# A hybrid decoder step on one core: wider transfers for the triangular inverses, convolution taps and state updates moved from GpSimd to VectorE, and narrow float32r products padded to 128 rows

## The chip, the cores and the metric

The kernel runs on one core of a Trainium2 chip. The metric is the time of one execution on the device, in microseconds. TensorE (PE) multiplies matrices, VectorE (DVE), ScalarE (ACT) and GpSimd (POOL) work on elements, and SyncE (SP) issues every DMA of this kernel. Results of TensorE go to PSUM, whose contents VectorE and ScalarE read.

## The reference, cut to what matters

One inference step of a two-layer decoder for a prompt of 512 tokens and 8 sample tokens, model width 2048, all in float32. Layer one holds a 31-tap convolution module and stick-breaking attention, the latter also over paged caches of 2048 past tokens for each of the 8 samples. Layer two is a gated DeltaNet with 16 query/key heads and 32 value heads of dimension 128. Both layers begin with one large input projection and end with an output projection, a residual and a layer norm.

The change is mostly in layer two. Its core, for the prompt in chunks and for the samples in one recurrent step, is:

```python
qkv, new_buf = _causal_depthwise_conv(qkv, conv_buf, conv_w)      # 4 taps, 8192 channels
qkv = silu(qkv)
# prompt: per chunk of c tokens
lmat = where(strict, einsum('bhnid,bhnjd->bhnij', kb, kc) * decay, 0.0)
tmat = triangular_solve(lmat + eye, eye, lower=True, unit_diagonal=True)
...
# samples: one step with the state s (8 samples, 32 heads, 128 x 128)
s = s * exp(g_t)[..., None, None]
delta = (v_t - einsum('bhkv,bhk->bhv', s, k_t)) * b_t[..., None]
s = s + einsum('bhk,bhv->bhkv', k_t, delta)
o = einsum('bhkv,bhk->bhv', s, q_t)
```

## The kernel before, in words

**Planner.** `build` doesn't call the engines directly. Each operation is recorded (`Sched.record`) with its dependencies, a cost from `Sched.cost` and a priority, and `Sched.flush` simulates the five engines and emits the operations in the order of the start times that it worked out. There is a flush at the end of each stage. On the chip every engine then runs its own list in that fixed order, and real semaphores hold it where an input is late. `sc.prio` shifts a priority; `-HP` comes first. SP's list holds every DMA, so a DMA that takes long to issue delays the ones behind it.

**Projections.** `gemm` loads a weight block (512 KB, `wr`), splits it into a high and a low part of type float32r (`wh` by ScalarE, `wl` by VectorE), splits the activations the same way (`uh`, `ul`), and adds up three products in PSUM (`pg`). These matmuls of 128 rows and 260 columns make up most of TensorE's work.

**Layer two.** The second flush region begins with `gates` and then `prepare(i)` for the 16 head pairs: two projections, a 4-tap convolution of each (`conv_c`), the products of keys with keys and queries (`kqh`, `kql`), a broadcast of the cumulated gates (`gr`, a product of `idr`, one column repeated, with `gst`, 64 rows), and the stores of what the scan needs into DRAM, tiles `sp0` to `sp15` (kq, kt, it, lt). Slots 5 and 6 of the seven hold the triangular matrices of the pair's two value heads.

**Inverses.** `inverses(b8, iv)` takes eight head pairs at once. It loads the 64 x 64 diagonal blocks of their triangular matrices, one block per partition (8 pairs x 2 heads x 4 chunks x 2 blocks = 128), into the tile `m`, inverts them on VectorE by 119 multiply-and-reduce steps (`tmp<-m`, then `m<-tmp`), and stores the blocks back. Batch 0 runs beside the preparation of pairs 8 to 15 and the first gate projections (`z`); batch 1 is a generator that is advanced in the background of the scan (`background`). Batch 1 uses the same tile `m`.

**Scan.** The next flush region goes over the 16 pairs: `values(i)` (two projections and `conv_c` for the values), `z_gates`, `scan(i)` (loads the four chunks `pk` from `sp`, finishes the inverse on TensorE and steps the prompt's state through the chunks), `samples(i)` (the recurrent step of the 8 samples), `normalise(i)` and the store of `y`. The tiles of this stage (`lb`: `oss`, `es`, `selr`, ...) take the memory that the preparation's tiles (`lk`) held, among them the `dd` buffers through which the gates `z` are stored.

**Samples.** `samples(i)` loads the pair's state `S` (1 MB), multiplies it on TensorE by a selection of keys and queries (`es`), sums the four column groups by `selr` (8 columns of weights, twice two products), works out the deltas on 8 partitions, replicates them with `repr` (8 rows, two products) into `dm`, and adds the outer products (`kx` x `dm`, 32 rows, two samples at a time into the PSUM tile `pl`, of which there is one buffer) to the state, which GpSimd has multiplied by the decay `egb` in one operation of 2048 columns. Then `S` is stored (`o_ds`) and its only buffer is free for the next pair.

**Other places.** In layer one, `scores(b)` replicates a query row by a product of 40 rows and 512 columns (`sel8`, `qrow`; 16 times in all), and `bcast_half` broadcasts four statistics columns by a product of 4 rows.

Of the kernel before, what the change touches and what calls it, by code (L numbers as in the profile page):

```python
# [38 lines left out]
class Sched:  # L39
# [79 lines left out]
    def region(self, ap):  # L119
# [24 lines left out]
        return rec, p0, p0 + dims[0][1], m  # L144

# [83 lines left out]
    def cost(self, eng, meth, args, kw, out, ins):  # L229
# [21 lines left out]
        if eng == "SP":  # L251
# [8 lines left out]
            few = any(x.space != bass.MemoryType.DRAM and x.shape[0] <= 8 for x in [out] + ins) and by > 20000  # L260
# [223 lines left out]
def build(tc, a, ctx):  # L484
# [173 lines left out]
    with ExitStack() as l0:  # L658
# [89 lines left out]
        qrow = lp.tile([40, H, P], F32R, name="qrow")  # L748
        sel8 = lp.tile([40, NB], F32R, name="sel8")
        S.copy(sel8, ident[0:40, 40:48])  # L750
        for j in (0, 32):
            S.copy(sel8[j:j + NB], ident[j:j + NB, j:j + NB])
        for g in range(2):
# [4 lines left out]
            S.copy(qg, qp[0:40])  # L758
# [464 lines left out]
    spill = [dr.tile([4, P, 7, P], F32, name=f"sp{i}") for i in range(GQ)]  # L1223
# [3 lines left out]
    with ExitStack() as l1:  # L1227
# [14 lines left out]
        idr = kp.tile([2 * NH, NH], F32R, name="idr")  # L1242
# [8 lines left out]
        def conv_c(g, psf, dst, win, s):  # L1251
# [30 lines left out]
        def prepare(i, lk):  # L1282
# [126 lines left out]
        def gates(gp_):  # L1409
# [28 lines left out]
            S.copy(gst, gc2)  # L1438
# [37 lines left out]
        with ExitStack() as l1a:  # L1476
            lk = sc.pool(l1a, "l1a", 1)
            gst = lk.tile([2 * NH, T], F32R, name="gst")
# [71 lines left out]
        selr = lb.tile([P, 2, NB], F32R, name="selr")  # L1550
        S.copy(selr, C("sel_kq").rearrange("p (j b) -> p j b", j=2))
        repr_ = lb.tile([NB, 2, 32], F32R, name="repr")
        S.copy(repr_, C("rep8", NB).rearrange("p (j r) -> p j r", j=2))
# [89 lines left out]
        def samples(i, dv, oss, lb):  # L1643
# [25 lines left out]
            qs = lb.tile([NB, 2, P], F32, name="qs")  # L1669
            for hd in range(2):  # L1670
                h = 2 * i + hd
                V.scalar_tensor_tensor(dl[:, hd, :], kp_[:, 0, hd, :], rows8[:, 0, h:h + 1], vr[:, hd, :], op0=ALU.mult, op1=ALU.add)
                V.tensor_scalar(dl[:, hd, :], dl[:, hd, :], rows8[:, 1, h:h + 1], None, op0=ALU.mult)
                S.activation(qs[:, hd, :], kp_[:, 1, hd, :], AF.Copy, scale=rows8[:, 2, h:h + 1])
            V.scalar_tensor_tensor(qs, dl, qk8[:, i:i + 1], qs, op0=ALU.mult, op1=ALU.add)
            for hd in range(2):
                V.scalar_tensor_tensor(vr[:, hd, :], qs[:, hd, :], 1.0 / P, qs[:, hd, :], op0=ALU.mult, op1=ALU.mult,
                                       accum_out=oss[0:NB, 8 + hd:9 + hd])

            dh = lb.tile([NB, 2, P], F32R, name="tmp1")  # L1680
            S.copy(dh, dl)
            dlo = lb.tile([NB, 2, P], F32R, name="el")
            V.tensor_tensor(dlo, dl, dh.bitcast(F32), op=ALU.subtract)
            rp = pm.tile([32, 256], F32, name="pd", bufs=1)
            for j, x in enumerate((dh, dlo)):
                PE.matmul(rp, repr_[:, j], x.rearrange("p h v -> p (h v)"), start=(j == 0), stop=(j == 1))
            dm = lb.tile([32, 256], F32R, name="dm")
# [3 lines left out]
            G.tensor_tensor(s, s, egb[:, :, 2 * i:2 * i + 2, None].broadcast_to([P, NB, 2, P]), op=ALU.mult)  # L1691
            for b2 in range(NB // 2):
                if b2 % 2 == 0:
                    kx = lb.tile([32, 4, P], F32R, name="kx")
                    V.tensor_tensor(kx, kw[:, None, :].broadcast_to([32, 4, P]),
# [4 lines left out]
                sv = s[:, 2 * b2:2 * b2 + 2].rearrange("p b h v -> p b (h v)")  # L1700
                V.tensor_tensor(sv, sv, up, op=ALU.add)
# [3 lines left out]
        def normalise(i, osb, qs, oss, zt, y, lb):  # L1705
# [16 lines left out]
            V.tensor_tensor(qs, qs, oss[0:NB, 8:10, None].broadcast_to([NB, 2, P]), op=ALU.mult)  # L1722
            op_ = pm.tile([P, 2, NB], F32, name="pd", bufs=1)
            for hd in range(2):
                PE.transpose(op_[:, hd, :], qs[:, hd, :], ident[0:NB, 0:NB])
# [194 lines left out]
```

## Time and profile before

| | |
|---|---|
| median of 3 runs | 3327.67 us (3323.73 to 3341.83) |
| the profiled execution | 3313.89 us |
| its span, first to last instruction | 3312.1 us |
| TensorE busy | 3108.7 us, 94% |
| VectorE busy | 2341.9 us, 71% |
| ScalarE busy | 1566.5 us, 47% |
| GpSimd busy | 342.6 us, 10% |
| DMA | 667.02 MB, mean 201 GB/s |

The span is what the rows of the trace are counted in. The profiled execution is faster than the median by 13.8 us. Busy time is a union of spans; matmuls are pipelined, so that a span reaches beyond the time at which the next one starts, and a TensorE at 94% is not at its peak. Layer one lies from 0 to about 1280 us, the preparation from there to about 1870, the scan from 1920 to about 2925, and the last projection behind it.

### The profile page before, as it was taken

To read this page: it belongs to the slowest core of one execution; us is meant where nothing else is said; L and a number is where in the kernel's file an instruction comes from. 1 tells how busy PE (TensorE), PEld (TensorE's weight loads), DVE (VectorE), ACT (ScalarE), POOL (GpSimd) and SP (SyncE) were. 2 spreads that over 40 slices of the span, in tenths; PEclk is the share of its full clock that TensorE was granted. 3 is DMA by queue.
4 is the path that set the end of the run, shared out by engine and by line. 5 is a ranking of instruction groups with operands and counts; after the bars stand their busy time and mean duration, and the time that the engine had idled before them with its cause. 6 is when DMAs were issued, how large, how long until landed. Compare 5 with 4: busy or idle time off the path is not lost. (4 is left out here: it accounts for less than half of the span.)

```text
span 3312.1 us, 65624 instructions
## 1 busy us (share of the span) xinstructions
PE 3108.7 (94%) x24496; PEld 2806.7 (85%) x24496; DVE 2341.9 (71%) x6214; ACT 1566.5 (47%) x2927; POOL 342.6 (10%) x301
## 2 busy tenths in 40 slices
PE   8999999989979999999999668999989999999997
PEld 5898888877867777999999667987878989999997
DVE  3487989787864485668999426998975766566755
ACT  2234344434552366777652124545444655554544
POOL 0000000000001011111110011111112110101111
PEclk9999999999979999999999888998989999999999
DMA  9978989998538886776653255544446545376764
GB/s 317 298 256 290 316 299 315 304 319 305 175 119 282 296 294 210 162 163 151 146 151 116 74 113 145 140 141 145 139 126 186 149 145 161 119 231 211 225 185 139
DMA packets 361586, 667.02 MB, mean 201 GB/s; under 512 B 103697, under 2 KB 216338, under 8 KB 357170
## 3 DMA queue, kind: packets, MB, share of 16 engines
q1 hardware_dynamic: 361266, 662.82, 65.4%
q8 instruction: 193, 3.16, 0.4%
q14 instruction: 127, 1.04, 0.1%
HBM read 574.95 MB, written 87.70 MB: 200 GB/s over the span
## 5 line engine op out<-in xcount | busy, mean ns | idle before, releaser
L418 PE MATMUL pg<-uh,wh 128*128 128x260 f32 (+1 forms) x6112 | 1343.9, 289 | 6.6 <-ACT uh L418 3.1
L418 PE MATMUL pg<-ul,wh 128*128 128x260 f32 (+1 forms) x6112 | 1339.8, 289 | 1.5 <-DVE ul L418 1.1
L418 PEld LDWEIGHTS pg<-uh,wh 128*128 128x128 f32 (+1 forms) x6112 | 998.3, 190 | 62.2 <-issue 46.6
L418 PEld LDWEIGHTS pg<-ul,wh 128*128 128x128 f32 (+1 forms) x6112 | 998.9, 190 | 56.1 <-issue 43.6
L418 PE MATMUL pg<-uh,wl 128*128 128x260 f32 (+1 forms) x6112 | 892.0, 289 | 0.0
L418 DVE TENSOR_TENSOR wl<-wr,wh 128x1024 fp32r<-128x1024 f32 (+3 forms) x508 | 618.7, 1218 | 382.6 <-PE pg L418 161.5
L418 ACT CAST wh<-wr 128x1024 fp32r<-128x1024 f32 (+3 forms) x508 | 511.4, 1007 | 791.9 <-PE pg L418 671.3
L418 PEld LDWEIGHTS pg<-uh,wl 128*128 128x128 f32 (+1 forms) x6112 | 793.2, 190 | 46.6 <-issue 39.2
L418 DVE SCALAR_TENSOR_TENSOR junk<-page,qbc 128x128 f32<-128x128 f32 x1024 | 222.6, 284 | 9.7 <-ACT qbc L418 6.2
L418 DVE TENSOR_TENSOR tmp<-m 128x224 f32<-128x224 f32 (+19 forms) x238 | 214.5, 901 | 4.5
L418 DVE SCALAR_TENSOR_TENSOR acc<-gp,conv_w_a,acc 128x512 f32<-128x512 f32 x240 | 181.0, 754 | 6.6 <-ACT acc L418 3.9
L418 ACT ACT_TABLE_LOAD x120 | 154.0, 1283 | 49.8 <-DVE rs L418 19.5
L418 DVE TENSOR_REDUCE m<-tmp 128x32 f32<-128x224 f32 (+19 forms) x238 | 130.7, 549 | 3.3
L418 POOL TENSOR_SCALAR ctap<-buf,conv_w_c 128x512 f32<-128x512 f32 x64 | 72.7, 1135 | 524.9 <-ACT buf L418 521.5
L418 POOL TENSOR_TENSOR cacc<-cacc,ctap 128x512 f32<-128x512 f32 x64 | 84.9, 1326 | 388.6 <-DVE cacc L418 340.8
L418 DVE SCALAR_TENSOR_TENSOR cacc<-buf,conv_w_c,cacc 128x512 f32<-128x512 f32 x128 | 99.9, 781 | 13.9 <-ACT cacc L418 9.6
L418 PE MATMUL pl<-wa,cpad 128*32 128x512 f32 x512 | 81.0, 604 | 5.8 <-DMA wa<-w_ada 5.6
L418 DVE DVE_READ_ACCUMULATOR junk<-page,qbc 128x1 f32 x1024 | 81.4, 79 | 0.0
L418 PE MATMUL pg<-yh,wh 128*128 128x260 f32 x320 | 79.1, 283 | 0.0
L418 PE MATMUL pg<-yl,wh 128*128 128x260 f32 x320 | 78.9, 283 | 0.0
L418 POOL TENSOR_TENSOR S<-S,egb 128x2048 f32<-128x2048 f32 x16 | 59.5, 3722 | 165.4 <-PE pd L418 165.4
L418 PE MATMUL pl<-page,wst 128*32 128x512 f32 x512 | 75.1, 611 | 0.2
(377 smaller groups left out, 3615.5 us busy)
## 6 DMA issues: line engine op xcount, KB each, us to landing
wr<-w_in_odd SPq DMA_DIRECT2D x194, 512.0 KB
page<-cache_k SPq DMA_DIRECT2D x128, 512.0 KB
wa<-w_ada SPq DMA_DIRECT2D x128, 512.0 KB
page<-cache_v SPq DMA_DIRECT2D x128, 512.0 KB
wr<-w_out_odd SPq DMA_DIRECT2D x128, 512.0 KB
wr<-w_in_even SPq DMA_DIRECT2D x94, 512.0 KB
page<-w_ada SPq DMA_DIRECT2D x128, 256.0 KB
pk<-sp SPq DMA_DIRECT2D x64, 448.0 KB
```

The lines of the kernel that those rows point to most:

```text
L418: o[2](*o[3], **o[4])
```

## The change

- `inverses` loads and stores blocks of 16 partitions (four head pairs, one value head, one diagonal block) instead of 4; the order of blocks on the partitions changes with it. For this the sixteen DRAM tiles `sp` become one tile `spa` of which `spill[i]` are slices, and the planner's `region` learns which parts of it an access touches. The planner's price for transfers of few partitions now holds up to 16 partitions.
- `conv_c` runs its three taps on VectorE; the GpSimd product and addition are gone.
- `samples` scales and adds the state in one VectorE operation per sample and head (16 of 128 columns per pair) instead of one GpSimd product and four additions.
- Products with fewer than 128 rows get operands with zero rows up to 128: `sel8`/`qrow`, `idr`/`gst`, the statistics broadcast, `repr` (its two products become one, with the low part on rows 32 to 39), `kx`/`dm`, and the transposes of `qs`. `selr` becomes 128 columns wide and one matrix for keys and queries, so that two products do the work of four. The fills are ScalarE copies with scale 0, made once.

```diff
@@ record / region / cost
-            return rec, lo, hi + 1, 1
+            return rec, lo, hi + 1, self.parts(rec["shape"], dims, off) if len(rec["shape"]) == 4 else 1
-            few = any(x.space != bass.MemoryType.DRAM and x.shape[0] <= 8 for x in [out] + ins) and by > 20000
+            few = any(x.space != bass.MemoryType.DRAM and x.shape[0] <= 16 for x in [out] + ins) and by > 20000
+    def parts(self, shape, dims, off):
+
+        per = shape[1] * shape[2] * shape[3]
+        dims = tuple(d for d in dims if d[0] % per)
+        key = (off % per, dims, "parts")
+        if key not in self.masks:
+            idx = np.array([off % per])
+            for s, c in dims:
+                idx = (idx[:, None] + s * np.arange(c)[None, :]).reshape(-1)
+            p, s, f = np.unravel_index(idx, shape[1:])
+            self.masks[key] = sum(1 << int(q) for q in np.unique((p // 64 * shape[2] + s) * 2 + f // 64))
+        return self.masks[key]
@@ bcast_half
-            PE.matmul(out[:, 256:260], col[0:4, 4 + n:5 + n].broadcast_to([4, P]), ident[0:4, 0:4], start=True, stop=True)
+            PE.matmul(out[:, 256:260], col[:, 4 + n:5 + n].broadcast_to([P, P]), ident[:, 0:4], start=True, stop=True)
@@ qrow, sel8, scores
-        qrow = lp.tile([40, H, P], F32R, name="qrow")
-        sel8 = lp.tile([40, NB], F32R, name="sel8")
-        S.copy(sel8, ident[0:40, 40:48])
+        qrow = lp.tile([P, H, P], F32R, name="qrow")
+        sel8 = lp.tile([P, NB], F32R, name="sel8")
+        S.activation(sel8, ident[:, 0:NB], AF.Copy, scale=0.0)
+        S.activation(qrow.rearrange("p h d -> p (h d)"), wst.rearrange("p g q r -> p (g q r)"), AF.Copy, scale=0.0)
...
-                PE.matmul(qp.rearrange("p j d -> p (j d)"), sel8[:, b:b + 1].broadcast_to([40, P]),
+                PE.matmul(qp.rearrange("p j d -> p (j d)"), sel8[:, b:b + 1].broadcast_to([P, P]),
@@ layer two
-    spill = [dr.tile([4, P, 7, P], F32, name=f"sp{i}") for i in range(GQ)]
+    spa = dr.tile([4 * GQ, P, 7, P], F32, name="sp")
+    spill = [spa[4 * i:4 * i + 4] for i in range(GQ)]
...
-            tap = lw.tile([P, T], F32, name="ctap")
-            G.tensor_scalar(tap, buf[:, 0:T], cwc[:, g, 0:1], 0.0, op0=ALU.mult, op1=ALU.add)
-            for t in (1, 2):
+            for t in range(3):
                 V.scalar_tensor_tensor(acc, buf[:, t:t + T], cwc[:, g, t:t + 1], acc, op0=ALU.mult, op1=ALU.add)
-            G.tensor_tensor(acc, acc, tap, op=ALU.add)
...
-                PE.matmul(gr.rearrange("p c f -> p (c f)"), idr[:, h:h + 1].broadcast_to([2 * NH, P]), gst, start=True, stop=True)
+                PE.matmul(gr.rearrange("p c f -> p (c f)"), idr[:, h:h + 1].broadcast_to([P, P]), gst, start=True, stop=True)
@@ inverses
-            for blk in range(2):
-                for i in range(8):
+            for i in (0, 4):
+                for blk in range(2):
                     for hd in range(2):
-                        p0 = blk * 64 + i * 8 + hd * 4
-                        dv = spill[8 * b8 + i][:, blk * 64:blk * 64 + 64, 5 + hd, blk * 64:blk * 64 + 64]
-                        blocks.append((m[p0:p0 + 4], dv))
+                        p0 = 64 * blk + 32 * hd + 4 * i
+                        c0, r = 4 * (8 * b8 + i), slice(64 * blk, 64 * blk + 64)
+                        blocks.append((m[p0:p0 + 16], spa[c0:c0 + 16, r, 5 + hd, r]))
@@ before the scan: selr, repr, kx, dhl, qs made once, filled with zeros
-        selr = lb.tile([P, 2, NB], F32R, name="selr")
-        repr_ = lb.tile([NB, 2, 32], F32R, name="repr")
+        fresh = lambda t, n: S.activation(t, zero.broadcast_to([P, n]), AF.Copy, scale=0.0)
+        selr = lb.tile([P, P], F32R, name="selr")
+        repr_ = lb.tile([P, P], F32R, name="repr")
+        kx = lb.tile([P, 4, P], F32R, name="kx")
+        dhl = lb.tile([P, 2, P], F32R, name="dhl")
+        qs = lb.tile([P, 2, P], F32, name="qs")
@@ samples
-            kp_ = pm.tile([NB, 2, 2, P], F32, name="pd", bufs=1)
-            for j in range(2):
-                for x in (eh, el):
-                    PE.matmul(kp_[:, j].rearrange("p h v -> p (h v)"), selr[:, j], x, start=(x is eh), stop=(x is el))
+            kp_ = pm.tile([P, 2, P], F32, name="pd", bufs=1)
+            for x in (eh, el):
+                PE.matmul(kp_.rearrange("p h v -> p (h v)"), selr, x, start=(x is eh), stop=(x is el))
...
-            for j, x in enumerate((dh, dlo)):
-                PE.matmul(rp, repr_[:, j], x.rearrange("p h v -> p (h v)"), start=(j == 0), stop=(j == 1))
+            PE.matmul(rp, repr_, dhl.rearrange("p h v -> p (h v)"), start=True, stop=True)
...
-            G.tensor_tensor(s, s, egb[:, :, 2 * i:2 * i + 2, None].broadcast_to([P, NB, 2, P]), op=ALU.mult)
...
-                sv = s[:, 2 * b2:2 * b2 + 2].rearrange("p b h v -> p b (h v)")
-                V.tensor_tensor(sv, sv, up, op=ALU.add)
+                for b in (2 * b2, 2 * b2 + 1):
+                    for hd in range(2):
+                        V.scalar_tensor_tensor(s[:, b, hd], s[:, b, hd], egb[:, b, 2 * i + hd:2 * i + hd + 1],
+                                               up[:, b % 2, P * hd:P * hd + P], op0=ALU.mult, op1=ALU.add)
@@ normalise
-                PE.transpose(op_[:, hd, :], qs[:, hd, :], ident[0:NB, 0:NB])
+                PE.transpose(op_[:, hd, :], qs[:, hd, :], ident)
```

## Rows read from the trace of the kernel before

**Rows 1.** Stretches: us; busy us (instructions) of each engine, clock, DMA share, GB/s

```profile
1520.00:1857.00 337.00, 335.44 (x2750) 329.65 (x2750) 324.30 (x582) 172.28 (x247) 34.19 (x39) 0.99 0.52 136
1924.00:2003.00 79.00, 68.17 (x486) 64.62 (x487) 20.45 (x25) 20.68 (x35) 7.33 (x8) 0.87 0.54 122
2003.00:2424.00 421.00, 390.43 (x2977) 351.96 (x2976) 387.01 (x835) 212.10 (x564) 62.68 (x45) 0.92 0.50 144
2424.00:2520.00 96.00, 80.51 (x632) 74.35 (x631) 47.37 (x114) 42.63 (x116) 11.06 (x10) 0.92 0.47 126
2520.00:2925.00 405.00, 396.69 (x3133) 361.38 (x3132) 277.00 (x673) 236.54 (x637) 59.16 (x46) 0.98 0.53 156
```

**Rows 2.** Timeline of VectorE: start us, duration us, operation [idle before, released by]

```profile
1856.10 0.91 DVE L418 MEMSET m<- 128x1024 f32 x1 [0.16 <-issue]
...
1918.12 0.10 DVE L418 MEMSET oss<- 128x10 f32 x2 [56.42 <-DMA z<-dd]
...
2011.39 0.17 DVE L418 TENSOR_TENSOR tmp<-m 128x8 f32<-128x8 f32 x1
```

**Rows 3.** Timeline of SP's queue, 1857 to 2003 us

```profile
1857.03 55.06 SPq L418 DMA_DIRECT2D sp<-m  x31
1912.19 1.56 SPq L418 DMA_DIRECT2D z<-dd  x1
...
2002.79 0.33 SPq L418 DMA_DIRECT2D m<-sp  x1
```

**Rows 4.** Timeline of TensorE behind the hole

```profile
1924.24 1.11 PE L418 MATMUL pm<-ct,vc 128*128 128x128 f32 x4 [52.31 <-ACT vc L418]
```

**Rows 5.** Timeline of SP's queue, the stores of batch 1

```profile
2423.86 3.19 SPq L418 DMA_DIRECT2D sp<-m  x3
...
2508.32 2.16 SPq L418 DMA_DIRECT2D S<-state_delta  x1
...
2513.40 1.19 SPq L418 DMA_DIRECT2D sp<-m  x1
```

**Rows 6.** DMA queue: packets, MB, share; 1875 to 1910, then 1300 to 1302

```profile
q1 hardware_dynamic: 5023, 1.27, 21.7%
...
q1 hardware_dynamic: 1140, 0.57, 98.5%
```

**Rows 7.** VectorE's groups, 2003 to 2424: count, busy us, mean ns, idle before

```profile
L418 DVE SCALAR_TENSOR_TENSOR cacc<-buf,conv_w_c,cacc 128x512 f32<-128x512 f32 x24 | 20.5, 853 | 0.3 <-ACT cacc L418 0.2
L418 DVE TENSOR_TENSOR S<-S,pl 128x512 f32<-128x512 f32 x28 | 18.9, 674 | 0.2 <-PE pl L418 0.2
...
L418 DVE SCALAR_TENSOR_TENSOR st<-st,gl,pm 128x128 f32<-128x128 f32 x42 | 12.7, 339 | 1.6 <-PE pm L418 1.5
...
L418 DVE COPY es<-kqd 128x8 f32<-128x8 f32 x15 | 8.1, 556 | 0.3 <-PE pd L418 0.2
```

**Rows 8.** GpSimd's groups, 2003 to 2424

```profile
L418 POOL TENSOR_TENSOR S<-S,egb 128x2048 f32<-128x2048 f32 x7 | 26.9, 3846 | 26.7 <-PE pd L418 26.7
```

**Rows 9.** Timeline of TensorE around a gate row product and a kx pair

```profile
1391.39 0.40 PE L418 MATMUL pg<-ul,wh 128*128 128x260 f32 x2
1391.63 0.28 PE L418 MATMUL pg<-uh,wh 128*128 128x260 f32 x1
1391.84 0.49 PE L418 MATMUL pd<-gst,idr 64*128 64x512 f32 x1
1392.26 0.39 PE L418 MATMUL pg<-uh,wh 128*128 128x260 f32 x1
1392.49 0.40 PE L418 MATMUL pg<-ul,wh 128*128 128x260 f32 x2
...
2642.40 0.50 PE L418 MATMUL pl<-dm,kx 32*128 32x256 f32 x2
2642.83 0.52 PE L418 MATMUL pg<-ul,wh 128*128 128x260 f32 x2
```

**Rows 10.** TensorE's groups, 1924 to 2925: the kx products

```profile
L418 PE MATMUL pl<-dm,kx 32*128 32x256 f32 x128 | 37.0, 373 | 20.6 <-DVE oss L418 9.4 <-DVE S L418 8.5 <-DVE osb L418 2.0
```

More of the change, by code (lines that the diff above doesn't have):

```diff
@@ L757, in build @@
             qg = qrow[:, g * 4:g * 4 + 4, :]
[L758 removed]
+            S.copy(qg[0:40], qp[0:40])
             V.tensor_tensor(qg[32:40], qp[32:40], qg[32:40].bitcast(F32), op=ALU.subtract)
@@ L1241, in build @@
         rq2 = kp.tile([P, GQ, 4], F32, name="rq2")
-        idr = kp.tile([2 * NH, NH], F32R, name="idr")
+        idr = kp.tile([P, NH], F32R, name="idr")
+        S.activation(idr, ident[:, 0:NH], AF.Copy, scale=0.0)
         kqd = kp.tile([P, GQ, 2, NB], F32, name="kqd")
@@ L1437, in gates @@
             Q.dma_start(gc2[lo], gcs)
-            S.copy(gst, gc2)
+            S.activation(gst, C("mask2").bitcast(F32)[:, 0:1].broadcast_to([P, T]), AF.Copy, scale=0.0)
+            S.copy(gst[0:2 * NH], gc2)
             V.tensor_tensor(gst[lo], gc2[lo], gst[lo].bitcast(F32), op=ALU.subtract)
@@ L1477, in build @@
             lk = sc.pool(l1a, "l1a", 1)
-            gst = lk.tile([2 * NH, T], F32R, name="gst")
+            gst = lk.tile([P, T], F32R, name="gst")
             gates(lk)
@@ L1549, in build @@
             G.memset(t, 0.0)
-        selr = lb.tile([P, 2, NB], F32R, name="selr")
-        S.copy(selr, C("sel_kq").rearrange("p (j b) -> p j b", j=2))
-        repr_ = lb.tile([NB, 2, 32], F32R, name="repr")
-        S.copy(repr_, C("rep8", NB).rearrange("p (j r) -> p j r", j=2))
+        zero = C("mask2")[:, 0:1]
+        fresh = lambda t, n: S.activation(t, zero.broadcast_to([P, n]), AF.Copy, scale=0.0)
+        flat3 = lambda t: t.rearrange("p j f -> p (j f)")
+        selr = lb.tile([P, P], F32R, name="selr")
+        fresh(selr, P)
+        repr_ = lb.tile([P, P], F32R, name="repr")
+        fresh(repr_, P)
+        for j in range(2):
+            S.copy(selr[:, 32 * j:32 * j + NB], C("sel_kq")[:, NB * j:NB * j + NB])
+            S.copy(repr_[32 * j:32 * j + NB, 0:32], C("rep8", NB)[:, 32 * j:32 * j + 32])
+        kx = lb.tile([P, 4, P], F32R, name="kx")
+        fresh(flat3(kx), 4 * P)
+        dhl = lb.tile([P, 2, P], F32R, name="dhl")
+        qs = lb.tile([P, 2, P], F32, name="qs")
+        for t in (dhl, qs):
+            fresh(flat3(t), 2 * P)
         def scan(i, vs, osb, oss, lb):
@@ L1675, in samples @@
-            V.scalar_tensor_tensor(qs, dl, qk8[:, i:i + 1], qs, op0=ALU.mult, op1=ALU.add)
+                S.activation(qs[0:NB, hd, :], kp_[32:32 + NB, hd, :], AF.Copy, scale=rows8[:, 2, h:h + 1])
+            V.scalar_tensor_tensor(qs[0:NB], dl, qk8[:, i:i + 1], qs[0:NB], op0=ALU.mult, op1=ALU.add)
             for hd in range(2):
-                V.scalar_tensor_tensor(vr[:, hd, :], qs[:, hd, :], 1.0 / P, qs[:, hd, :], op0=ALU.mult, op1=ALU.mult,
+                V.scalar_tensor_tensor(vr[:, hd, :], qs[0:NB, hd, :], 1.0 / P, qs[0:NB, hd, :], op0=ALU.mult, op1=ALU.mult,
@@ L1687, in samples @@
-            dm = lb.tile([32, 256], F32R, name="dm")
+            S.copy(dhl[0:NB], dl)
+            V.tensor_tensor(dhl[32:32 + NB], dl, dhl[0:NB].bitcast(F32), op=ALU.subtract)
+            rp = pm.tile([P, 256], F32, name="pd", bufs=1)
+            PE.matmul(rp, repr_, dhl.rearrange("p h v -> p (h v)"), start=True, stop=True)
+            dm = lb.tile([P, 256], F32R, name="dm")
             S.copy(dm, rp)
@@ L1690, in samples @@
             Q.dma_start(kw, krd[:, i, :])
-            G.tensor_tensor(s, s, egb[:, :, 2 * i:2 * i + 2, None].broadcast_to([P, NB, 2, P]), op=ALU.mult)
             for b2 in range(NB // 2):
                 if b2 % 2 == 0:
-                    kx = lb.tile([32, 4, P], F32R, name="kx")
-                    V.tensor_tensor(kx, kw[:, None, :].broadcast_to([32, 4, P]),
+                    V.tensor_tensor(kx[0:32], kw[:, None, :].broadcast_to([32, 4, P]),
                                     C("mask_b", 32)[:, 2 * b2:2 * b2 + 4, None].broadcast_to([32, 4, P]), op=ALU.mult)
@@ L1721, in normalise @@
                                        _pn(zt[hd])[:, :, 0:256], op0=ALU.mult, op1=ALU.mult)
-            V.tensor_tensor(qs, qs, oss[0:NB, 8:10, None].broadcast_to([NB, 2, P]), op=ALU.mult)
-            op_ = pm.tile([P, 2, NB], F32, name="pd", bufs=1)
+            V.tensor_tensor(qs[0:NB], qs[0:NB], oss[0:NB, 8:10, None].broadcast_to([NB, 2, P]), op=ALU.mult)
+            op_ = pm.tile([P, 2, P], F32, name="pd", bufs=1)
             for hd in range(2):
-                PE.transpose(op_[:, hd, :], qs[:, hd, :], ident[0:NB, 0:NB])
+                PE.transpose(op_[:, hd, :], qs[:, hd, :], ident)
             for hd in range(2):
-                V.scalar_tensor_tensor(d8(y[hd]), as8(op_[:, hd, :]), gnw, d8(zt[hd]), op0=ALU.mult, op1=ALU.mult)
+                V.scalar_tensor_tensor(d8(y[hd]), as8(op_[:, hd, 0:NB]), gnw, d8(zt[hd]), op0=ALU.mult, op1=ALU.mult)
         def values(i):
```

9 lines of the change are left out of this document (1 added, 8 removed).

## The prediction

> **What bounds the kernel now.** I read the table of stretches first, then the timelines of the places where it shows a hole, then the groups by shape. The stretches [rows 1] show the change's territory, layer two. While head pairs 0 to 15 are prepared, TensorE is busy 335 of 337 us and VectorE 324: VectorE runs the first batch of triangular inverses beside the preparation, and both engines are full. From 2003 to 2424 us (head pairs 0 to 7 scanned, second batch of inverses in the background) VectorE has 387 of 421 us and TensorE 390. From 2520 to 2925 (pairs 8 to 15, no inverses) TensorE has 397 of 405 and VectorE only 277. Between these lie two poor stretches, 1924 to 2003 (TensorE 68 of 79, VectorE 20) and 2424 to 2520 (81 of 96 and 47).
>
> The hole itself stands between the first two stretches. Batch 0's last operation, a memset, ends at 1857 [rows 2]; from then on SP issues 31 of its 32 stores back to back for 55 us, and the store of the last gate tile, z, stands behind them at 1912 [rows 3]. The second stage's tiles reuse that gate tile's memory, so VectorE waits 56.42 us for it to land [rows 2], and TensorE, out of work at 1872, waits 52.31 us [rows 4]. Then batch 1's 32 loads go out among the weight loads until 2003 [rows 3], and its first multiply runs only at 2011.39 [rows 2]. At the other end of batch 1 the 32 stores take from 2424 to 2513, and the state load of pair 8, which starts the next stretch, comes at 2508 [rows 5].
>
> **The change part by part.** *Transfers.* A store is now 4 partitions of 64 x 64 floats: 256 runs of 256 bytes, 32 stores, 8192 packets. In 35 us amid the hole 5023 packets went, 143 per us, at a DMA share of 21.7%, which is 3.5 of 16 engines [rows 6]: four engines work, close to full, at 28 ns a packet. The stores of preparation, which span 128 partitions, show 570 packets per us at 98.5% [rows 6], again 28 ns per packet and engine, and those packets are twice as large. So the limit is the engine's time per packet, and a transfer of 16 partitions that spreads over 16 engines should carry 8192 packets in 8192/570 = 14.4 us instead of 57. Bounds: 14.4 us, and 57 us if the four engines are not what limits. I take 16, near the row with the same time per packet. The Trainium skill (SBUF — State Buffer, Door 1: The DMA port swizzle) says that four consecutive partitions share one of 16 ports, so 16 of them reach only four; at its 435 GB/s for all ports that would be an estimated 109 GB/s, and 19 us for these 2.1 MB. By it the hole would shrink 3 us less; no run here shows it.
>
> *Resumption.* Before, z goes out at 1912.19 and VectorE resumes at 1918.12, 5.9 us later [rows 2, 3]. After: 1857 + 16 + 5.9 = 1879, 39 us sooner, if batch 0 ends when it did. It ends later by the VectorE work added to the eight pairs beside it (16 convolutions x 0.85 us = 13.6) and sooner by what GpSimd's locks and the gate products give back; I take 3 us later, so 36 us. Five fills on ScalarE now stand before the first convolution of this stage, 1280 columns in all; at 512 columns per 0.85 us they are 2 us, inside the rounding.
>
> *Loads.* The eight new loads carry the same 8192 packets; interleaved with weights I allow 25 us (bounds 16 and 93) from the resumption to the first multiply of batch 1, where it was 93.3 (1918.12 to 2011.39). Batch 1 starts near 1907, 104 us sooner.
>
> *VectorE takes GpSimd's work.* Per pair: two convolutions with one more tap, 2 x 0.85 = 1.7 us, and the state update, 16 multiply-adds of 128 columns at 0.339 (nearest row: st, same operands) = 5.4 in place of 4 x 0.674 = 2.7 [rows 7]. So +4.4. Given back: what GpSimd blocked. The 15 copies es of 8 columns average 0.556 us [rows 7] where another operation on 8 columns takes 0.17 [rows 2], and GpSimd's own product lasts 3.8 us [rows 8]; that is 0.8 per pair, bounds 0 and 8 (all of GpSimd's 62.7 us in this stretch [rows 1]). I take +3.5 per pair, 25 over the seven pairs that ran beside batch 1. At 92% busy the batch then needs 412 + 27 = 439 us, from 1907 to 2346 instead of 2424: 78 us sooner. Its stores, 84 us from their start to pair 8's state load, need 16 plus what SP interleaves; with 20 to 84 as bounds I take 45. VectorE alone would let pair 8 start 78 + 39 = 117 us sooner.
>
> *TensorE.* A narrow product pays three times. The gate row product of 512 columns starts 0.21 us after the matmul ahead (dense: 0.12), takes 0.42, and the next one needs 0.23 [rows 9]: 0.62 us more than if it weren't there. Full rows: 512 columns at the dense 0.12 per 260 is 0.24. Saved 0.38, for 32 of them, and for 16 of the same shape in layer one. A pair of kx products takes 0.43 for two [rows 9] and, with the same 0.20 of switching, 0.63 against 0.24: 0.39 saved, four times per head pair. The two repr products become one (0.41 each at most by the same rows, against 0.12: 0.7), four selr become two (0.24). Together 2.5 us a head pair. Here a rule speaks against the change: the Trainium skill (TensorE: Matmul & The Clock Gate, Why this matters for your kernels) says that a single K=32 matmul takes as long as a K=128 one and that the gain lies in running such tiles side by side. By it only the switching, 0.20 each, would be saved, and this term would halve to some 1.2 us a pair. The trace disagrees: 0.42 for 512 columns at 64 rows against a dense 0.12 for 260.
>
> TensorE's own bound for pairs 0 to 7: its 539 busy us from 1924 to 2520 [rows 1] less 8 x 2.5 = 519, from 1888 on at its 98% of the last stretch, ends 2418 instead of 2520: 102 us. Two engines both near full, each executing in a fixed order, will not reach either bound, 117 or 102; I take **85 us** up to pair 8, which holds all terms so far. Its bounds are 36 (the hole alone) and 102.
>
> *Pairs 8 to 15.* TensorE bounds, 8 x 2.5 = 20 us; VectorE has 128 us to spare for its +28. But each state update now holds the one PSUM buffer for 4 x 0.339 = 1.36 us where it held it 0.67, and kx products already waited 20.6 us [rows 10]. I take **15**, bounds 0 and 20.
>
> *Layer one.* 16 products of qrow x 0.38 = **6**, bounds 0 and 10 with the statistics broadcasts of 4 rows, whose cover is that TensorE is the full engine there. The extra zero rows cost fills on ScalarE, once each, ScalarE being half busy (212 of 421) [rows 1]. One DRAM tile for all pairs instead of sixteen I cost at nothing: the stores of one tile already go out back to back without waiting for landings [rows 3].
>
> Sum: 85 + 15 + 6 = 106 us. The profiled execution is 3313.89 us (span 3312.1), 13.8 below the median of the runs, 3327.67. Counted from the profile that is 3208; I forecast the median, 3327.67 - 106 = 3222 us. On its own this case runs from 3185 (102 + 20 + 10) to 3245.
>
> **The rivals.** *Only the hole closes.* Batch 1 starts sooner but VectorE, with more work in the stage where it is full already, gives nothing more: 36 + 15 + 6 = 57, 3270 us. For it: VectorE and TensorE are both over 90% in that stage. Against it: VectorE had 20 us of work in the 79 from 1924, time that batch 1 can now use.
>
> *The transfers stay as slow.* If the limit is common to all engines, hole, loads and end of batch 1 stay, VectorE's +27 stands against TensorE's 21: 3305 to 3340, no change. The 21.7% speaks against it.
>
> *The state update stalls TensorE (slower).* The mechanism: one PSUM buffer, which TensorE needs again after four VectorE operations instead of one; kx products stand in order ahead of the dense ones. The worst price is that all four rounds of 1.36 + 0.4 us are waited out, 7 us a pair, 113 us in 16, and VectorE's +27 in the first half: 3327.67 - 106 + 140 = 3360. It decides from 106/16 = 6.6 us a pair. Against it: the same ping-pong at half the length cost 20.6 us in all, 1.3 a pair.
>
> **How the numbers follow.** Chances: forecast 0.63, only the hole 0.20, transfers as slow 0.09, stalled update 0.08. The likeliest gives 3222. The range 3170 to 3290 holds the first two and a little beyond the first one's bounds; it leaves out the last two, 0.17. A measurement here tells from no change about 0.5%, 17 us. Faster: 0.63 + 0.20 + 0.01 of the third = 0.84; same 0.08; slower 0.08.
>
> **What would show it right or wrong.** Right: 8 stores that leave SP within some 16 us with DMA share near full, VectorE's wait for z under 15 us, batch 1's first multiply within 30 us of the resumption, pair 8's state load some 85 us sooner, and dense spacing of 0.12 us around the former narrow products. Wrong: stores still of 55 us in sum at a share of 22%; VectorE at 95% or more with TensorE below 90% in pairs 0 to 7; idle time ahead of kx several us a pair. A new order of the work, which the kernel's planner works out from its own costs, could also move layer one by more than the 6 us that I give it.

## The result, and the profile after

The changed kernel took 3224.11 us (median of 4 runs, 3205.37 to 3229.8) beside 3325.7 for the kernel before (4 runs, 3319.95 to 3341.83): ratio 0.9674, 95% interval 0.9629 to 0.972, so faster by 102 us. The forecast was 3222. Run again five times, beside a kernel before of 3312.67 us, it gave 0.9704 (0.9686 to 0.9721). The profiled execution took 3229.8 us, its span is 3228.0: 84 us below the profile of before. It is the slowest of its four runs, and the profile of before (3313.89) is faster than all four runs beside it, so the profiles hold 84 of the 102 us. Two single runs of kernels further down, of 10190.62 and 3290.12 us, show a granted clock of 0.27 and 0.87 where the other runs of the same kernels have 0.97 or more; they enter no ratio and move the medians by less than 1 us. The total came out as forecast; its parts did not.

The table of stretches, cut where the rows of before were cut [rows 1] (us, then busy us and count of each engine, granted clock, DMA share, GB/s):

```profile
1504.00:1830.00 326.00, 321.18 (x2658) 319.32 (x2659) 317.54 (x609) 176.77 (x252) 1.21 (x12) 0.99 0.53 138
1870.00:1914.00 44.00, 30.08 (x228) 27.68 (x227) 11.15 (x19) 11.35 (x24) 0.20 (x2) 0.85 1.12 142
1914.00:2352.00 438.00, 429.52 (x3534) 405.97 (x3535) 418.11 (x1009) 243.13 (x633) 1.52 (x15) 0.97 0.51 151
2352.00:2457.00 105.00, 100.06 (x762) 94.79 (x761) 59.60 (x147) 45.97 (x108) 0.30 (x3) 0.90 0.68 187
2457.00:2836.00 379.00, 352.53 (x2636) 318.84 (x2636) 242.26 (x691) 211.69 (x584) 1.01 (x10) 0.89 0.43 134
```

The reader is to see three things. The poor stretch ahead of batch 1 is 44 us long and no longer 79. From batch 1's first multiply to its last, VectorE is now 95% busy (418 of 438) and TensorE 98%. And the last stretch got worse: TensorE has 26 us idle in 379, where it had 8 in 405, and its granted clock fell from 0.98 to 0.89.

The hole, on VectorE's timeline (answers to [rows 2]):

```profile
1832.94 0.91 DVE L431 MEMSET m<- 128x1024 f32 x1 [0.16 <-issue]
...
1864.68 0.10 DVE L431 MEMSET oss<- 128x10 f32 x2 [12.01 <-DMA z<-dd]
...
1913.77 0.11 DVE L431 MEMSET m<- 128x64 f32 x1 [22.16 <-DMA m<-sp]
1913.92 0.17 DVE L431 TENSOR_TENSOR tmp<-m 128x8 f32<-128x8 f32 x1
```

Batch 0 ends 23 us sooner, not 3 later. From its last memset to VectorE's resumption it is 31.7 us, where it was 62.0. Batch 1's first multiply comes at 1913.92, 97.5 us sooner. On SP's queue (answers to [rows 3]) the eight stores and z now stand like this:

```profile
1833.88 0.94 SPq L431 DMA_DIRECT2D sp<-m  x2
1835.38 2.66 SPq L431 DMA_DIRECT2D wr<-w_in_odd  x1
1838.10 17.84 SPq L431 DMA_DIRECT2D sp<-m  x6
1856.04 5.34 SPq L431 DMA_DIRECT2D z<-dd  x2
```

The DMA rows from 1835 to 1852, amid them and with the 512 KB weight block `wr` among the stores, answer to [rows 6]:

```profile
DMA packets 5310, 1.84 MB, mean 109 GB/s; under 512 B 5181, under 2 KB 5181, under 8 KB 5309
...
q1 hardware_dynamic: 5309, 1.83, 74.6%
```

That is 5181 small packets in 17 us, 305 per us against 143 before. In the profile with the transfers alone (next section) no weight block goes among the stores, and there 4239 small packets went in the 12 us from 1856, 353 per us at a share of 72.8%: 2.5 times as many as before, not four times. At 353 the 8192 packets need 23 us; SP had issued the eight stores 22 us after the first, the weight block included.

Two full-row products on TensorE's timeline, a gate row product and a kx pair (answers to [rows 9]):

```profile
1381.61 0.40 PE L431 MATMUL pd<-gst,idr 128*128 128x512 f32 x1
1381.85 0.41 PE L431 MATMUL pg<-ul,wh 128*128 128x260 f32 x2
...
2443.05 0.41 PE L431 MATMUL pl<-dm,kx 128*128 128x256 f32 x2
2443.30 0.40 PE L431 MATMUL pg<-ul,wh 128*128 128x260 f32 x2
```

Each hands on after 0.24 and 0.25 us, as forecast, where the pattern of before took 0.42 and 0.43 and a slow start around it. VectorE's groups from batch 1's first multiply to its last, 1914 to 2352 (answers to [rows 7]):

```profile
L431 DVE SCALAR_TENSOR_TENSOR cacc<-buf,conv_w_c,cacc 128x512 f32<-128x512 f32 x45 | 33.5, 745 | 0.0
L431 DVE SCALAR_TENSOR_TENSOR S<-S,egb,pl 128x128 f32<-128x128 f32 x116 | 32.6, 340 | 0.6 <-PE pl L431 0.4
...
L431 DVE COPY es<-kqd 128x8 f32<-128x8 f32 x16 | 1.9, 170 | 2.2 <-PE pd L431 2.2
```

The multiply-adds cost 0.340 each as taken, but a tap fell from 0.853 to 0.745 us and an es copy from 0.556 to 0.170.

### The profile page after: what moved, and what is told of

It reads as the page before. It is cut to its first block, busy times and chain, and to the rows that moved or that the text cites. A ratio compares the mean times of both kernels' runs of the same rounds, so it can differ in the third digit from the quotient of the medians.

```text
span 3228.0 us, 65519 instructions
## 1 busy us (share of the span) xinstructions
PE 3072.7 (95%) x24448; PEld 2800.0 (87%) x24448; DVE 2346.4 (73%) x6470; ACT 1578.2 (49%) x2942; POOL 128.3 (4%) x157
## 4 chain that ended last, share of the span: by engine, by line
PE 84%; DVE 7%; DMA 6%; ACT 1%; SPq 1%; issue 1%; POOLq 0%; ACTq 0%; POOL 0%; DVEq 0%
PE pg L431 66%; PE pm L431 9%; PE pl L431 6%; PE pd L431 2%; SPq L431 1%; DVE wl L431 1%; DVE junk L431 1%; DMA S<-state_delta 1%; DMA page<-cache_k 1%; DMA wa<-w_ada 1%; DVE blk L431 1%; DVE acc L431 1%; DVE S L431 1%; DMA o_ds<-S 1%; DMA m<-sp 0%
## 5 line engine op out<-in xcount | busy, mean ns | idle before, releaser
L431 PE MATMUL pg<-uh,wl 128*128 128x260 f32 (+1 forms) x6112 | 880.6, 287 | 0.2
L431 DVE TENSOR_TENSOR tmp<-m 128x224 f32<-128x224 f32 (+19 forms) x238 | 200.8, 844 | 4.0
L431 DVE SCALAR_TENSOR_TENSOR cacc<-buf,conv_w_c,cacc 128x512 f32<-128x512 f32 x192 | 143.2, 746 | 13.8 <-ACT cacc L431 12.0
L431 DVE DVE_READ_ACCUMULATOR junk<-page,qbc 128x1 f32 x1024 | 90.2, 88 | 0.0
L431 DVE SCALAR_TENSOR_TENSOR S<-S,egb,pl 128x128 f32<-128x128 f32 x256 | 71.9, 341 | 5.7 <-PE pl L431 5.2
L431 ACT ACTIVATE jk<-osb 128x128 f32<-128x128 f32 x128 | 39.7, 310 | 54.9 <-DVE osb L431 53.9
```

The costliest lines, as they stand in the source:

```text
L431: o[2](*o[3], **o[4])
```

## The experiments

The kernel before ran at 3313, 3313 and 3316 us beside the three groups of runs (medians), so kernels of different groups are compared by their ratios to it; 0.003 is 10 us.

**The parts, one at a time.** Transfers alone, added to the kernel before:

```
-            return rec, lo, hi + 1, 1
+            return rec, lo, hi + 1, self.parts(rec["shape"], dims, off) if len(rec["shape"]) == 4 else 1
...
-                        blocks.append((m[p0:p0 + 4], dv))
+                        blocks.append((m[p0:p0 + 16], spa[c0:c0 + 16, r, 5 + hd, r]))
```

> The kernel before with one part of the change: the inverses' transfers over 16 partitions (8 loads and 8 stores a batch). GpSimd's work and the narrow products stay as before. Theory 1 (the transfers carry the gain): the stores leave in some 18 us instead of 57, VectorE resumes some 38 us sooner, batch 1 starts some 100 us sooner and pair 9 some 75 us sooner; time 3326 - 75 = 3250, 3235 to 3265. Rival (only the hole closes, VectorE is full already beside batch 1): pair 9 some 40 us sooner, 3285. Rival (the other parts carry most): over 3300.

Measured: 3232.16 us, 0.9753 (0.973 to 0.9776), 81 us faster. Pair 9's state load comes 85.5 us sooner, and batch 1's first multiply 81 us sooner, where 100 was expected. By the ratio, which stands for 3244 us beside 3326, theory 1 holds.

The same part undone in the changed kernel (the lines above the other way round):

> The changed kernel with one part undone: the inverses' transfers are again of 4 partitions (32 loads and 32 stores a batch). Theory 1: the hole of some 52 us and the late start of batch 1 return, and what is left of the gain is that of the full rows less VectorE's extra work: 3300 to 3325. Rival (the work moved from GpSimd and the full rows gain by themselves in pairs 0 to 7): under 3285.

Measured: 3272.53 us, 0.9874 (0.9846 to 0.9901). The transfers are worth 56 us from this side (0.9704 against 0.9874), 81 from the other; the first 1.3% come without them. The rival (under 3285) was right: something else in the change gains by itself. The next two runs say what.

```
+            G.tensor_tensor(s, s, egb[:, :, 2 * i:2 * i + 2, None].broadcast_to([P, NB, 2, P]), op=ALU.mult)
...
-                for b in (2 * b2, 2 * b2 + 1):
-                    for hd in range(2):
-                        V.scalar_tensor_tensor(s[:, b, hd], s[:, b, hd], egb[:, b, 2 * i + hd:2 * i + hd + 1],
-                                               up[:, b % 2, P * hd:P * hd + P], op0=ALU.mult, op1=ALU.add)
+                sv = s[:, 2 * b2:2 * b2 + 2].rearrange("p b h v -> p b (h v)")
+                V.tensor_tensor(sv, sv, up, op=ALU.add)
```

> The changed kernel with one part undone: the states' update is again GpSimd's product and four VectorE adds of 512 columns. Full rows, taps on VectorE and wide transfers stay. Theory 1 (in pairs 8 to 15 the four multiply-adds hold the one PSUM buffer and make TensorE wait ahead of the kx products): the stretch from pair 9's state load to pair 15's, 316 us in the changed kernel and 308.5 before, falls to 290 to 300, the granted clock there stays at 0.95 or more, and the time is 3205 to 3215. Rival (the loss there comes from the clock or the order of the work, whatever the update): the stretch stays at 310 to 320 and the time at 3220 to 3230. Rival (GpSimd's product blocks VectorE more than it saves): 3235 or more.

Measured: 3217.08 us, 0.9708 (0.9687 to 0.9729), the same as the changed kernel. Pair 9 to pair 15 took 308.2 us where the changed kernel took 316.0 and 290 to 300 was expected, at a granted clock of 0.90: theory 1, that the loss there comes from the four multiply-adds that make TensorE wait, falls.

All full rows undone, the rest of the change kept (selr, repr, kx, dm, qs, gst, idr, qrow, sel8 and the statistics' broadcast as before):

```
-        kx = lb.tile([P, 4, P], F32R, name="kx")
+                    kx = lb.tile([32, 4, P], F32R, name="kx")
...
-            gst = lk.tile([P, T], F32R, name="gst")
+            gst = lk.tile([2 * NH, T], F32R, name="gst")
```

> The changed kernel with one part undone: all narrow products have their 4 to 64 rows again, as before. Wide transfers and VectorE's taps and updates stay. Theory 1 (2.5 us of TensorE a head pair, TensorE the bound in both halves): pairs 0 to 7 end 15 to 20 us later and the time is 3250 to 3265. Rival (only switching is saved, half of it): 3237 to 3245. Rival (TensorE has idle time where these products stand, so they cost nothing): 3220 to 3228.

Measured: 3207.3 us, 0.9672 (0.9652 to 0.9693), no slower than the changed kernel: of the three only the last, that these products cost nothing, is left. So in the change as made the full rows gained nothing, where the forecast had 46 us. And beside the transfers alone (0.9753) the taps and the update on VectorE gained 27 us, where the forecast charged VectorE for them.

**Why taps and update gain.** VectorE's groups from its resumption to pair 15, transfers alone:

```profile
L431 DVE SCALAR_TENSOR_TENSOR cacc<-buf,conv_w_c,cacc 128x512 f32<-128x512 f32 x62 | 49.7, 802 | 19.8 <-DMA m<-sp 13.5 <-ACT cacc L431 6.2
L431 DVE TENSOR_TENSOR S<-S,pl 128x512 f32<-128x512 f32 x60 | 40.7, 678 | 11.9 <-PE pl L431 10.4 <-issue 1.1
...
L431 DVE COPY es<-kqd 128x8 f32<-128x8 f32 x32 | 30.3, 981 | 30.2 <-PE pd L431 29.9 <-POOL es L431 0.2
```

and with taps and update on VectorE, narrow rows (the kernel of the last run):

```profile
L431 DVE SCALAR_TENSOR_TENSOR cacc<-buf,conv_w_c,cacc 128x512 f32<-128x512 f32 x93 | 69.1, 743 | 3.5 <-ACT cacc L431 2.7
L431 DVE SCALAR_TENSOR_TENSOR S<-S,egb,pl 128x128 f32<-128x128 f32 x240 | 67.2, 339 | 8.3 <-PE pl L431 8.2
...
L431 DVE COPY es<-kqd 128x8 f32<-128x8 f32 x32 | 4.1, 177 | 22.5 <-PE pd L431 22.2 <-POOL es L431 0.3
```

Taps and update add 19.4 and 26.5 us. The 32 copies es alone give back 26.2, and VectorE's whole sum in that stretch is 690.1 us beside 690.8: all 46 us come back, 3.1 a pair. That is what GpSimd had held VectorE up. The mean of 0.98 us hides two kinds of copies. With transfers alone, 24 of the 32 take some 0.17 us, and the 8 that begin while GpSimd's product `S<-S,egb` runs last until it ends. One of them, and the product:

```profile
2054.23 2.57 DVE L431 COPY es<-kqd 128x8 f32<-128x8 f32 x1
2053.14 3.62 POOL L431 TENSOR_TENSOR S<-S,egb 128x2048 f32<-128x2048 f32 x1 [3.10 <-PE pd L431]
```

In the four profiles that have the product 24 copies begin inside it, and each ends 0.03 to 0.07 us behind it. `el<-pd,tmp`, which reads PSUM, takes 0.42 us inside it as elsewhere. The Trainium skill (SBUF — State Buffer, SBUF: two separate sides) states that VectorE and GpSimd share a port pair as an exclusive lock, held for a whole instruction; the copies agree, at 2.5 to 3.7 us when begun inside the product and 0.17 otherwise.

Which of GpSimd's two jobs was it? Each moved alone, beside the wide transfers (the hunks of the diff for conv_c, or for the update):

> The kernel before with wide transfers and the convolutions' third tap on VectorE; the states' product stays on GpSimd and all narrow rows as before. Beside it: wide transfers alone 0.9753, with taps and update on VectorE 0.9672. Theory A (GpSimd's product over the state blocks VectorE's copies es, 1.0 us instead of 0.17, and is what costs): 0.974 to 0.978, es still near 1.0 us. Rival (the taps carry the 27 us): 0.967 to 0.970. By the forecast (1.7 us of VectorE a pair, added where VectorE is full): 0.979.

> The kernel before with wide transfers and the states' update in sixteen VectorE multiply-adds of 128 columns; the convolutions' first tap stays on GpSimd and all narrow rows as before. Theory A (as with the taps alone: GpSimd's product is what blocks VectorE): es falls from 0.98 to near 0.17 us, VectorE's sum stays the same, 0.967 to 0.970. Rival (the taps carry the gain): 0.974 to 0.977. By the forecast (2.7 us of VectorE a pair less 0.8 given back): 0.979.

Measured: 3223.48 us, 0.9726 (0.9706 to 0.9745), and 3227.34 us, 0.9724 (0.9699 to 0.9749): some 9 us each, neither well apart from the 0.9753 of the transfers alone, and both together 27 (the intervals, 6 to 8 us to either side, leave a plain sum of the two possible). The copies es took 0.36 us with the taps moved and 0.17 with the update moved, though 0.77 in the run with the update put back, where GpSimd has the same product to do as with the taps moved: the order decides how many copies begin inside it, 2 and 6 of 32. By the time neither theory holds, and how the two share the gain in the scan stays open. In the preparation, where GpSimd has only the taps, the taps moved bring batch 0's last multiply from 1849 to 1837 us, and the update moved leaves it at 1852.

**Why full rows gain nothing.** First the rows alone, with the order of all instructions held:

```
-                    PE.matmul(up[:, q, :], kx[:, 2 * (b2 % 2) + q, :], dm, start=True, stop=True)
+                    PE.matmul(up[:, q, :], kx[0:32, 2 * (b2 % 2) + q, :], dm[0:32], start=True, stop=True)
...
-            rows = 32 if k <= 32 else 64 if k <= 64 else 128
+            rows = 128 if ins[1].dtype == F32R or meth != "transpose" and n == 4 and k == 4 else 32 if k <= 32 else 64 if k <= 64 else 128
```

> The changed kernel unchanged, on one chip with the kernels beside it, since the chips differ by some 0.4% in the time of the kernel before. Ratio to the kernel before 0.9674, between 0.964 and 0.971, by every theory; it is the measure for the others.

> The changed kernel with the order of all instructions kept, instruction by instruction, and only the rows of the products cut back on the chip: qrow and its selector 40 rows, gst and idr 64, repr and dhl 64, kx and dm 32, the statistics' broadcast 4. The planner's cost is held at that of full rows, so that the order can't move. Theory A (the rows are worth what the forecast says, and the planner's new order threw it away): 32 x 0.38 + 16 x 0.38 + 16 x (4 x 0.39 + 0.3) = 48 us, bounds 30 and 50, slower than the changed kernel. Theory B (TensorE only waits elsewhere for the time that full rows save, or loses it to the granted clock): within 12 us of the changed kernel. Theory C (switching alone, half of it): some 24 us slower.

Measured: 3214.16 us, 0.9704, and 3268.5 us, 0.986 (0.983 to 0.989): narrow rows cost 54 us in this order, the 48 worked out from the forecast's prices and a little more. Between the two profiles 9.3 us are lost by the time `gst` is filled at the head of layer two (layer one, 16 products; forecast 6), 11.9 more by VectorE's resumption (32 gate products; forecast 12), 29.7 more by pair 15 (samples). At a held order the mechanism and its prices stand. What a planner makes of them is the other half:

> The changed kernel with the full rows undone in the samples alone (kx and dm, repr and dhl, selr, qs as before); the planner works out its own order. The gate rows and layer one keep full rows. Theory A (the samples' full rows cost time in the planner's order: 22 us in the profiles between VectorE's resumption and pair 15, beside the kernel with all rows undone): 10 to 22 us faster than the changed kernel. Theory B (they neither cost nor gain): within 5 us of it. By the forecast (2.1 us a pair gained): 30 us slower.

> The changed kernel with full rows in the gate products alone (gst and idr); samples and layer one as before. Theory A: the 32 gate products give the 11 us that lie between the two profiles at VectorE's resumption, and layer one's full rows cost some 4 us by the last page: 10 to 15 us faster than the kernel with all rows undone, ratio 0.963, and the fastest so far. Rival: what the gate rows give is lost again later: ratio 0.966 to 0.969. For layer one: the last page's load comes 3 to 5 us sooner than with its full rows, or (forecast) no sooner.

Measured: 3199.87 us, 0.9661 (0.9643 to 0.9679), and 3203.97 us, 0.9674 (0.9656 to 0.9693). With the samples' rows undone the kernel is faster than the changed one, by 14 us: theory A. Gate rows alone bring VectorE's resumption 12.4 us sooner than with all rows undone, as forecast, but the end is no sooner (0.9674 beside 0.9672): theory A's 0.963 is missed and the rival holds. Layer one's full rows move nothing that can be told: `gst` is filled between 1279 and 1287 us in the seven profiles with them and between 1280 and 1287 in the six without (the kernel before among them).

The planner costs an F32R product of 64 rows or fewer at 0.833 ns a column and a full one at 0.417. VectorE's groups from its resumption to batch 1's last multiply, the changed kernel run again (1861 to 2342 us):

```profile
L431 DVE TENSOR_TENSOR wl<-wr,wh 128x1024 fp32r<-128x1024 f32 x55 | 67.2, 1221 | 13.1 <-PE pg L431 8.0 <-ACT wh L431 3.4 <-issue 0.6
...
L431 DVE SCALAR_TENSOR_TENSOR vdl<-vn,dec,vdh 128x128 fp32r<-128x128 f32 x64 | 20.3, 344 | 0.0
```

and with the samples' rows undone (1856 to 2310 us):

```profile
L431 DVE TENSOR_TENSOR wl<-wr,wh 128x1024 fp32r<-128x1024 f32 x50 | 61.0, 1220 | 12.0 <-PE pg L431 7.3 <-ACT wh L431 3.5 <-issue 0.7
...
L431 DVE SCALAR_TENSOR_TENSOR vdl<-vn,dec,vdh 128x128 fp32r<-128x128 f32 x56 | 17.4, 344 | 0.0
```

With cheap samples the planner puts pair 7's scan (eight more vdl) and five more weight splits ahead of batch 1's last multiply, on a VectorE that is full; that multiply comes 27 us later counted from the resumption (481 against 454). More work stands between it and the batch's last memset, so that the batch itself ends 40 us later (498 against 459). Pairs 8 to 15 need batch 1. While they wait, TensorE takes dense products that would have stood beside the later pairs. Counted between state loads (us, dense products pg):

| kernel | pair 8 | pair 9 | pair 10 | pair 11 | pair 9 to pair 15 |
|---|---|---|---|---|---|
| changed, run again | 82.0, 469 | 46.9, 192 | 52.5, 192 | 57.1, 109 | 313.4 |
| samples' rows undone | 62.9, 317 | 47.7, 244 | 53.2, 276 | 47.3, 196 | 309.2 |
| planner told they are slow | 64.1, 257 | 45.9, 227 | 52.3, 270 | 44.0, 226 | 297.4 |

So the last experiment keeps every full row on the chip and gives back only the cost:

```
+                    sc.thin = True
                     PE.matmul(up[:, q, :], kx[:, 2 * (b2 % 2) + q, :], dm, start=True, stop=True)
+                    sc.thin = False
...
-            rows = 32 if k <= 32 else 64 if k <= 64 else 128
+            rows = 32 if k <= 32 or self.thin else 64 if k <= 64 else 128
```

> The changed kernel with every full row kept on the chip; only the planner is told that the samples' kx and repr products still cost what narrow rows cost, so that it lays out an order like that of the kernel with the samples' rows undone. Theory A (not the rows but the order that the planner makes of their lower cost loses the time: pair 7's scan and five more weight splits put ahead of batch 1's last operation): batch 1 ends near 2310 instead of 2342 to 2352, pair 8's period falls from 82 to 91 us to some 63, and the time is 10 to 33 us below the changed kernel, ratio 0.960 to 0.967. Theory B (full rows themselves lower TensorE's granted clock in pairs 8 to 15 or leave it waiting): no better than the changed kernel, 0.969 to 0.972.

Measured: 3192.75 us, 0.9624 (0.9609 to 0.964), 27 us below the changed kernel and the fastest here; it beats both. Batch 1's last multiply comes at 2317, and pair 8's period is 64 us: theory A. By ratio: the changed kernel's order with full rows 0.9704, with all rows narrow 0.986; an order planned for narrow samples with full rows 0.9624, and with the samples' products as before, in a similar order but not the same, 0.9661. So the samples' rows are worth some 12 us there, and the order itself, with the same instructions on the chip, 27. That the order costs this is shown; that it does so by batch 1's late end and the dense products spent meanwhile is read from the table and was not tried by itself.

What happens in pair 11 is seen in its row of stretches, the changed kernel run again:

```profile
2539.20:2596.30 57.10, 47.23 (x258) 38.48 (x258) 32.28 (x96) 27.11 (x78) 0.20 (x2) 0.69 0.35 105
```

and with the planner told:

```profile
2541.30:2585.30 44.00, 43.68 (x359) 40.61 (x360) 30.64 (x92) 26.04 (x72) 0.10 (x1) 1.00 0.50 161
```

With 100 matmuls fewer the pair takes 13 us more. The first 12.8 us of the first of the two, and TensorE's timeline further on in it, show why:

```profile
2539.20:2552.00 12.80, 12.80 (x60) 11.04 (x59) 4.90 (x7) 4.03 (x10) 0.20 (x2) 0.50 0.37 131
```

```profile
2565.79 0.61 PE L431 MATMUL pm<-r,pk 128*128 128x128 f32 x4
...
2569.24 0.38 PE L431 MATMUL pm<-vdl,th 128*128 128x256 f32 x1 [1.24 <-DVE vdl L431]
...
2572.54 1.22 PE L431 MATMUL pm<-r,pk 128*128 128x128 f32 x4 [0.72 <-ACT osb L431]
...
2585.77 0.77 PE L431 MATMUL pl<-dm,kx 128*128 128x256 f32 x2 [1.31 <-DVE S L431]
...
2588.43 0.77 PE L431 MATMUL pl<-dm,kx 128*128 128x256 f32 x2 [1.89 <-DVE oss L431]
```

From 2567.6 to 2593.6 no dense product is left to fill the waits of the pair's own chain through VectorE and ScalarE. The granted clock is 0.69 over the pair: 0.50 or 1.00 for most of it, which are the two levels of 1.2 and 2.4 GHz. It is 0.50 from 2572.5 to 2590, and four r products take 1.22 us there where the four at 2565.79, the last beside dense work, take 0.61. It is also 0.50 in the pair's first 12.8 us, though TensorE is busy throughout: they follow the waits at the end of pair 10 (0.6 to 2.7 us each, 2529 to 2538), and two dense products take 0.64 us there instead of 0.40. So the pair's chain runs slower for want of work that has nothing to do with it, and the dense work behind such waits runs slower too.

**The rival of the stalled update, once more,** on the kernel with the samples' rows undone:

```
-                up = pm.tile([P, 2, 256], F32, name="pl", bufs=1)
+                up = pm.tile([P, 2, 256], F32, name="pd" if b2 % 2 else "pl", bufs=1)
```

> The changed kernel with the samples' full rows undone, and the PSUM buffer of the states' update taken in turn from two names instead of one, so that kx products needn't wait for the four multiply-adds of the round before. Theory A (they hardly wait: TensorE's idle time ahead of kx is 0.7 us a pair): 0 to 8 us faster than with one buffer, ratio 0.963 to 0.967. Rival (the forecast's stalled update: up to 1.4 us a round, three rounds a pair, 16 pairs): 30 to 65 us faster.

Measured: 3194.63 us, 0.9633 (0.9617 to 0.9648), beside 0.9661 with one buffer: at most some 9 us, and the intervals overlap. A stall of 30 to 65 us isn't there.

## Why the prediction was right, step by step

The forecast, "transfers free VectorE, batch 1 starts sooner, pair 8 starts sooner", was the mechanism: transfers alone give 81 of the 102 us (56 when they are taken out of the changed kernel). That the total lies 2 us from the forecast is luck. Its three terms and VectorE's, measured in the profiles, where 98 - 14 gives the 84 us between them:

- **85 us up to pair 8:** 98, by pair 9's state load (2555.0 to 2457.3). Pair 8's own state load, the forecast's sign, comes 142 us sooner (2508.3 to 2366.7), but it no longer waits behind batch 1, and pair 8 then takes 91 us instead of 47.
  - *Transfers:* 570 packets per us was too good. It is 353 with nothing else in the queue, and the time from batch 0's last memset to VectorE's resumption shrank by 30 us, not 39. The rows of other transfers, with all 128 partitions, didn't carry over to 16: 16 engines at 72.8% for 353 packets per us is 33 ns a packet, not 28. The Trainium skill's page that the prediction weighed (SBUF — State Buffer, Door 1: The DMA port swizzle) allows 109 GB/s here; 353 packets of 256 bytes are 90 GB/s, below that bound, where the forecast's 146 lay above it.
  - *Batch 0's end:* 23 us sooner instead of 3 later. Its last multiply stands at 1851 before, 1849 with transfers alone, 1839 with taps and update too, 1830 with the rows. That is GpSimd's share, here the taps', and the gate rows'. The forecast had named both without a price and set them below 13.6 us of added work.
  - *Loads:* 49 us to the first multiply, not 25, inside the bounds of 16 to 93. These misses nearly cancel: batch 1 starts 97.5 us sooner (104 forecast).
  - *Batch 1:* from the first multiply to the last memset it takes 455 us, not 439 (412 before), with one more pair's scan in it (48 st against 42), so it ends 55 us sooner and not 78. From there to pair 9's state load it is 88 us where it was 131: 43 us gained behind the batch, where the forecast had 39.
- **VectorE's +3.5 us a pair** is the term of this sum that was mis-sized: it is about 0. Given back were 3.1 us a pair, not 0.8; the bound of 8 held it. The es mean of 0.556 that the forecast read in pairs 0 to 7 [rows 7] is 1.00 over all sixteen in the same trace, and GpSimd's product holds up other operations too, such as a weight split that took 3.7 us instead of 1.2.
- **15 us in pairs 8 to 15:** wrong. From pair 9's state load to the end the profile lost 13.6 us (757.1 to 770.7). The step that failed is "TensorE bounds, 8 x 2.5 = 20 us". The price of a product was right, but the order did not stay: the planner spent the dense products earlier, and TensorE's waits and the lower granted clock took more than the rows gave.
- **6 us in layer one:** 1.0 lost by the time `gst` is filled. At a held order the rows are worth 9.3 there. Why the planner's order with narrow rows is no slower in layer one was not tried. The forecast's last sentence, that a new order could move layer one by more than its 6, fits this, and it held for pairs 8 to 15 too, where it was not said.

So the total was met by errors that cancel: 46 us of rows that did not arrive, against VectorE's work, which came free, and an earlier end of batch 0. The forecast's own bounds were also added up wrongly: 102 + 20 + 10 taken from 3327.67 is 3196, not 3185, and 36 alone gives 3292, not 3245. The measured time lies inside either pair. Of the signs that were to show it right, VectorE's wait for z (12.0 us, under 15) and the dense spacing around the former narrow products came. The stores (22 us at a share of 75%, not 16 near full) and batch 1's first multiply (49 us behind the resumption, not within 30) missed.

Of the rivals, "only the hole closes" falls (batch 1 starts 97.5 us sooner, the hole gives 30). "Transfers stay as slow" falls too, though they are 2.5 times as fast and not four times. "The state update stalls TensorE" falls: idle time ahead of the kx products, from 1871 to 2836, is 15.7 us in the changed kernel against 20.6 before [rows 10]. As to the Trainium skill's rule on short contractions (TensorE: Matmul & The Clock Gate, Why this matters for your kernels), by which only the switching would be saved, half of the term: at a held order 54 us appeared, the whole term and not half of it, so the measurement goes against it for these float32r products.

## What to carry to other kernels

Where a planner lays out the order, a cheaper instruction is also a new order: measure the saving at a held order and the new order by itself, since here the first was 54 us and the second ate it. Independent dense work is a store that fills the waits of a dependent chain; here it also went with the clock, 1.00 in a pair that had it and 0.69 in one that lacked it. Do not let it be spent while everything waits for something else. Before charging an engine for work taken over from GpSimd, look for short operations of that engine with odd means, such as 0.98 us for 8 columns, see whether the long ones end where a GpSimd operation ends, and count what they give back.

## What the runs showed of the hardware

A copy of 8 columns on VectorE that began while GpSimd multiplied 2048 columns in SBUF lasted until that product ended, 24 of 24 times, up to 3.7 us; the others took 0.17. Stores of 16 partitions with 256-byte packets moved 353 packets per us at a DMA share of 72.8%, those of 4 partitions 143 at 21.7%. A head pair with 258 matmuls at a granted clock of 0.69 took longer, 57.1 us, than one with 359 at 1.00, 44.0 us.
